# Stick-breaking attention: the earliest key block turned over and multiplied with V for 64 queries only

## The chip, the cores and the metric

The kernel runs on the 8 cores of one Trainium2 chip. The metric is the device time of the slowest core, in microseconds. Most executions agree within 0.3%. Some fall into a slower state, in which the cores of one die, or of both, are granted a lower clock; those executions are named slow, and only fast ones are compared with fast ones.

## The reference

One layer of a decoder: a SwiGLU half step, a short convolution beside stick-breaking attention, a second SwiGLU half step, an embedding gated per position, norms. Batch 4, sequence 8192, width 1024, 8 heads of 128. The part concerned is the attention:

```python
# A[t,s] = sigmoid(z_ts) * prod_{s<j<t} (1 - sigmoid(z_tj)), z = q.k / sqrt(dh), s < t
mask = k_pos[None, :] < q_pos[:, None]                      # strict causal
log_1m_beta = jnp.where(mask, jax.nn.log_sigmoid(-z), 0.0)
tail = lax.cumsum(log_1m_beta, axis=3, reverse=True) - log_1m_beta
a = jnp.where(mask, jnp.exp(jax.nn.log_sigmoid(z) + tail), 0.0)
out = jnp.einsum('bhqk,bhkd->bhqd', a, vf)
```

The weight of a key is what is left of a stick after all later keys have broken off their share. Each key leaves a factor 1 - sigmoid(z), so with the reference's random inputs nothing that fp32 can hold is left after some 200 keys. That is why the kernel need not look at all 8192 keys.

## The kernel before

A core computes half a sequence of one batch: 8 tiles of 512 positions. A slot is one head and one block of 128 queries; a core has 8 tiles x 8 heads x 4 blocks = 256 slots. Each slot looks at 320 keys: the 128 of its own block, the 128 before them, and 64 more. Slots are run as a pipeline of three stages between the matmuls of the large projections:

```python
WIN = 320
...
def attn1(self, s, q, kpieces, L, diag, init):
    ...                                  # scores: matmuls of q with L keys, into PSUM bank 4 or 5
    self.act(nbt.v(0, 0, L), z, AF.Sigmoid, scale=-QS)           # 1 - beta
    ...                                  # scan from the latest key to the earliest:
    #   rt = max(rt * (1 - beta), mask); mask row q is 1 where own-block key s >= q
    A = self.ats[s % 3]
    pad = -L % 128
    self.tt(A.v(0, pad, pad + L), Rt.v(0, 1, L + 1), Rt.v(0, 0, L), ALU.subtract)   # the weights
    return Rt.v(0, 0, 1)                 # what is left before the earliest key

def attn2(self, s, nb):                  # turn the weights over, 128 x 128 at a time
    T = self.PS[6]
    ...
    for b in range(nb):
        ins = self.nc.tensor.transpose(T[:, b * 128:(b + 1) * 128], A.v(0, b * 128, (b + 1) * 128).ap, self.ident.v(0).ap)
    ...
    self.act(self.att[s % 2].v(0, 0, nb * 128), View(T[:, 0:nb * 128], self.psres[6]), AF.Copy)

def attn3(self, s, vpieces, qb, start, stop, o):    # times V, summed over key blocks in PSUM
    ...
    for b, vv in enumerate(vpieces):
        ...
        ins = self.nc.tensor.matmul(O[:, qb * 128:(qb + 1) * 128], lhsT=vv.ap, rhs=at.v(0, b * 128, (b + 1) * 128).ap, ...)

def slot(self):
    ...
    end = b.attn1(s, X.q.v(h, qb * 128, (qb + 1) * 128), self.kpieces(X, h, qb), WIN, True, None)
    f = b.fend.v(0, self.base + s, self.base + s + 1)
    b.op(b.POOL, lambda: b.nc.gpsimd.tensor_copy(out=f.ap, in_=end.ap), [end], [f])
```

The 320 weights lie behind 64 columns of zeros, so that they fill three blocks of 128. The last two lines belong to a guard. For each slot GpSimd saves the column of what is left of the stick; before the end it is tested whether all of it is exactly zero. If one value is not, the whole layer is computed again with all keys:

```python
def flags():
    b.op(DVE, lambda: nc.vector.tensor_scalar(out=flg.v(0).ap, in0=b.fend.v(0).ap, scalar1=0.0, scalar2=None,
                                              op0=ALU.not_equal), [b.fend.v(0)], [flg.v(0)])
    ...                                  # maximum along the row, then a matmul with ones counts partitions
...
guard = nc.If(cond[0] >= 0) if force_general else nc.If(cond[0] > 0)
with guard:
    b.barrier()
    ...
    general(b, nc, S, A, B, x_d, p_d, out_d, h1_d, kT_d, v_d, uhalo, ring_off, at)
```

In this document the program up to the guard is the short path, and what the guard adds behind it, the computation with all keys, is the general path.

## Time and profile before

| | before |
|---|---|
| fast executions, with the first measurement | 3516.31, 3517.28, 3518.05 us |
| slow one, left out | 3659.46 us |
| TensorE busy | 97% of the span |
| attention: scores, transposes, V products | about 1% each of the chain that ended last |
| GpSimd busy | 6% |

The busy line, the chain, one slot on the timeline and the waits are shown in the prediction below. Two lines it does not show matter for the comparison. First the copy of the turned-over weights out of PSUM, from the page's groups (busy us, mean ns; then the idle time ahead and its releaser), then the guard's copies and test on core 3, from the list of the instructions on the guard's tile (duration in ns as smallest/median/largest, first and last start in us):

```profile
L281 ACT ACTIVATE sb_at_93<-ps 128x384 bf16<-128x384 bf16 x128 | 62.9, 491 | 158.5 <-PE ps L659 158.5
```

```profile
L741 POOL COPY sb_fend<-sb_rt_87 x128: 183/183/511, 384.4 to 3101.4; 128x1 f32<-128x1 f32 x128
...
L1189 DVE TENSOR_SCALAR sb_flg<-sb_fend x1: 286/286/286, 3117.7 to 3117.7; 128x256 bf16<-128x256 f32 x1
```

### The profile page before, as it was taken

Reading aid. Unit: us, or ns where it says so; the run is one execution under the profiler, and the core shown is the slowest. Engines: PE = TensorE matmul, PEld = TensorE weight load, DVE = VectorE, ACT = ScalarE, POOL = GpSimd, SP = SyncE. Lnnn points to the kernel's source line nnn. Section 1 sums busy time; section 2 is a strip of 40 time slices with the busy share of each in tenths; the row PEclk is TensorE's granted clock in tenths of the full one; section 3 lists DMA queues with packets and bytes.
Section 4 is the critical chain, followed back from the end, with each engine's and each line's share of the span. In section 5 each row is a group of like instructions: output and inputs, shape, how many; then the busy total and the mean of one; then the engine's idle time right before and its main releaser. Section 6 shows DMA issues by size and latency. Waiting matters only on the chain.

```text
span 3513.5 us, 50834 instructions; the slowest of 8 cores (3506.3 to 3513.5 us)
## 1 busy us (share of the span) xinstructions
PE 3401.3 (97%) x17714; PEld 1639.0 (47%) x17714; DVE 1564.1 (45%) x2461; ACT 1038.4 (30%) x2024; POOL 196.3 (6%) x479
## 2 busy tenths in 40 slices
PE   6999999999999999999999999999999999999995
PEld 3555545444444455444444444544444445544453
DVE  3224376522552367541544337652255236754234
ACT  3112424312331244321333142531233124432113
POOL 0000111100000000100000000010000000010000
PEclk9999999999999999999999999999999999999997
DMA  8565746786533321342223422152232332133231
GB/s 179 127 136 149 156 103 149 175 204 138 126 92 118 122 71 61 102 138 66 86 75 117 131 79 73 55 162 76 68 95 82 119 127 73 61 103 114 72 109 49
DMA packets 98817, 381.03 MB, mean 108 GB/s; under 512 B 11136, under 2 KB 16512, under 8 KB 93440
## 3 DMA queue, kind: packets, MB, share of 16 engines
q1 hardware_dynamic: 68304, 253.95, 21.8%
q0 software_dynamic: 30256, 123.75, 16.8%
q8 instruction: 150, 2.46, 0.3%
q14 instruction: 107, 0.88, 0.1%
HBM read 346.19 MB, written 93.85 MB: 125 GB/s over the span
## 4 chain that ended last, share of the span: by engine, by line
PE 93%; DVE 2%; ACT 2%; DMA 1%; issue 1%; DVEq 0%; SPq 0%; ACTq 0%; POOLq 0%
PE ps L253 85%; PE ps L271 5%; PE ps L673 1%; PE ps L659 1%; ACT L281 1%; PE ps L626 1%; DMA sb_xA<-x_in 0%; DMA sb_ring<-w_out 0%; DMA sb_ring<-w_in1g 0%; DMA sb_ring<-w_in1u 0%; DVE sb_t_80 L288 0%; DVE sb_hB L288 0%; DVE sb_rt_87 L646 0%; DVE sb_t_82 L288 0%; ACT sb_t_81 L281 0%
## 5 line engine op out<-in xcount | busy, mean ns | idle before, releaser
L253 PE MATMUL ps<-sb_uA,sb_ring 128*128 128x512 bf16 x4448 | 994.3, 380 | 18.0 <-DVE sb_phalo L285 8.4
L253 PE MATMUL ps<-sb_uB,sb_ring 128*128 128x512 bf16 x4448 | 990.3, 379 | 3.8 <-DVE sb_mB L285 2.8
L253 PEld LDWEIGHTS ps<-sb_uA,sb_ring 128*128 128x128 bf16 x4448 | 432.8, 98 | 525.3 <-issue 26.5
L253 PEld LDWEIGHTS ps<-sb_uB,sb_ring 128*128 128x128 bf16 x4448 | 433.6, 98 | 510.4 <-issue 7.1
L253 PE MATMUL ps<-sb_hidB,sb_ring 128*128 128x512 bf16 (+2 forms) x1584 | 312.8, 357 | 5.6 <-DVE sb_t_81 L288 5.6
L253 PE MATMUL ps<-sb_hidA,sb_ring 128*128 128x512 bf16 x1408 | 309.3, 379 | 0.5 <-DMA sb_ring<-w_out 0.5
L253 PEld LDWEIGHTS ps<-sb_hidB,sb_ring 128*128 128x128 bf16 x1584 | 149.3, 99 | 164.4 <-issue 6.4
L253 PEld LDWEIGHTS ps<-sb_hidA,sb_ring 128*128 128x128 bf16 x1408 | 137.7, 98 | 165.4 <-issue 1.0
L646 DVE TENSOR_TENSOR_SCAN sb_rt_87<-sb_nb_85,sb_mask 128x320 f32<-128x320 f32 x128 | 105.5, 824 | 210.9 <-ACT sb_nb_85 L281 186.4
L281 ACT ACTIVATE sb_t_81<-ps 128x512 f32<-128x512 f32 (+3 forms) x176 | 101.6, 578 | 271.2 <-PE ps L253 235.3
L281 ACT ACTIVATE sb_t_83<-ps 128x512 f32<-128x512 f32 (+3 forms) x175 | 101.3, 579 | 260.3 <-PE ps L253 244.8
L281 ACT ACTIVATE sb_t_80<-ps 128x512 f32<-128x512 f32 (+4 forms) x148 | 85.3, 576 | 257.9 <-PE ps L253 257.2
L281 ACT ACTIVATE sb_t_82<-ps 128x512 f32<-128x512 f32 (+3 forms) x147 | 84.4, 574 | 247.4 <-PE ps L253 247.4
L281 ACT ACTIVATE sb_sqA<-sb_hA 128x512 f32<-128x512 f32 x105 | 66.1, 629 | 289.3 <-DVE sb_accA L285 254.6
L281 ACT ACTIVATE sb_sqB<-sb_hB 128x512 f32<-128x512 f32 (+2 forms) x112 | 67.5, 602 | 273.7 <-DVE sb_accB L285 245.7
L646 DVE TENSOR_TENSOR_SCAN sb_rt_88<-sb_nb_86,sb_mask 128x320 f32<-128x320 f32 x128 | 105.3, 822 | 64.0 <-ACT sb_nb_86 L281 31.1
L253 PE MATMUL ps<-sb_mA,sb_ring 128*128 128x512 bf16 x512 | 116.4, 379 | 0.0
L281 ACT ACTIVATE sb_at_93<-ps 128x384 bf16<-128x384 bf16 x128 | 62.9, 491 | 158.5 <-PE ps L659 158.5
L281 ACT ACT_TABLE_LOAD x63 | 80.8, 1283 | 66.8 <-PE ps L253 43.8
L285 DVE TENSOR_TENSOR sb_hidB<-sb_t_80,ps 128x512 bf16<-128x512 f32 x47 | 32.3, 687 | 128.1 <-PE ps L253 110.6
L253 PE MATMUL ps<-sb_mB,sb_ring 128*128 128x512 bf16 x384 | 88.8, 379 | 0.0
L281 ACT ACTIVATE sb_at_92<-ps 128x384 bf16<-128x384 bf16 x128 | 62.5, 488 | 84.3 <-PE ps L659 83.1
(358 smaller groups left out, 3386.5 us busy)
## 6 DMA issues: line engine op xcount, KB each, us to landing
sb_ring<-wb_out SPq DMA_DIRECT2D x56, 704.0 KB, 4.3
sb_ring<-wb_in1g SPq DMA_DIRECT2D x33, 512.0 KB, 4.0
sb_ring<-wb_in1u SPq DMA_DIRECT2D x33, 512.0 KB, 4.0
sb_ring<-wb_in2g SPq DMA_DIRECT2D x33, 512.0 KB, 3.6
sb_ring<-wb_in2u SPq DMA_DIRECT2D x33, 512.0 KB, 4.4
sb_ring<-w_out POOLq DMA_DIRECT2D x16, 704.0 KB, 9.7
wb_out<-sb_ring SPq DMA_DIRECT2D x16, 704.0 KB, 6.4
h_s<-sb_hA POOLq DMA_DIRECT2D x8, 1024.0 KB, 5.9
```

Of the source, the lines that this page charges most:

```text
L253: ins = self.nc.tensor.matmul(ps.ap, lhsT=l.ap, rhs=r.ap, start=(t == 0), stop=(t == n - 1), skip_group_check=True)
L271: ins = self.nc.tensor.matmul(ps.ap, lhsT=l.ap, rhs=r.ap, start=(t == 0), stop=(t == n - 1), skip_group_check=True)
L281: self.op(self.ACT, lambda: self.nc.scalar.activation(out=out.ap, in_=in_.ap, func=func, scale=scale, **kw), [in_, *extra], [out])
L285: self.op(self.DVE, lambda: self.nc.vector.tensor_tensor(out=out.ap, in0=a.ap, in1=b.ap, op=alu), [a, b], [out])
L626: ins = self.nc.tensor.matmul(Z[:, c0:c0 + kv.ap.shape[-1]], lhsT=q.ap, rhs=kv.ap, start=(n == 0), stop=(n == len(kpieces) - 1), skip_grou ...
L646: self.op(self.DVE, lambda: self.nc.vector.tensor_tensor_scan(out=rv.ap, data0=nv.ap, data1=mv.ap, initial=iv, op0=ALU.mult, op1=ALU.max), ...
L659: ins = self.nc.tensor.transpose(T[:, b * 128:(b + 1) * 128], A.v(0, b * 128, (b + 1) * 128).ap, self.ident.v(0).ap)
L673: ins = self.nc.tensor.matmul(O[:, qb * 128:(qb + 1) * 128], lhsT=vv.ap, rhs=at.v(0, b * 128, (b + 1) * 128).ap, start=(start and b == 0), ...
```

## The change

Of the 64 earliest keys of a window, queries 64 to 127 of the block are to see nothing any more: they keep 256 keys and the first 64 queries keep 320. The block that holds the 64 earliest keys is then turned over for 64 queries, not 128, and multiplied with V for 64 columns. The transposes of the kernel before turn over whole blocks of 128 x 128; to turn over fewer queries, they become matmuls with the identity, of which 64 columns are used for that block. Scores, sigmoid, scan and subtraction stay at 320 keys.

The guard must follow: for queries 0 to 63 (partitions 0 to 63) what is left before column 0 has to be zero, for queries 64 to 127 what is left before column 64. So two columns are saved per slot, and each half of the partitions is tested on its own column.

```diff
+NQ = WIN - 256
-            if r == 6:
-                t = g.enter_context(nc.psum_tensor(f"ps{r}", [128, 1024], BF16))
   (bank 6 is fp32 like the others)
-        for b in range(nb):
-            ins = self.nc.tensor.transpose(T[:, b * 128:(b + 1) * 128], A.v(0, b * 128, (b + 1) * 128).ap, self.ident.v(0).ap)
+        for b, n in pieces:
+            ins = self.nc.tensor.matmul(T[:, c:c + n], lhsT=A.v(0, b * 128, (b + 1) * 128).ap,
+                                        rhs=self.ident.v(0, 0, n).ap, start=(c == 0), stop=True, skip_group_check=True)
+            c += n
 ...
-        self.act(self.att[s % 2].v(0, 0, nb * 128), View(T[:, 0:nb * 128], self.psres[6]), AF.Copy)
+        self.act(self.att[s % 2].v(0, 0, c), View(T[:, 0:c], self.psres[6]), AF.Copy)
 ...
-            ins = self.nc.tensor.matmul(O[:, qb * 128:(qb + 1) * 128], lhsT=vv.ap, rhs=at.v(0, b * 128, (b + 1) * 128).ap,
+            ins = self.nc.tensor.matmul(O[:, qb * 128:qb * 128 + n], lhsT=vv.ap, rhs=at.v(0, c, c + n).ap,
 ...
-        for blk in range(qb - 2, qb + 1):
+        for blk in (qb - 1, qb, qb - 2):
 ...
-            b.attn2(s - 2, 3)
+            b.attn2(s - 2, [(1, 128), (2, 128), (0, NQ)])
 ...
-            f = b.fend.v(0, self.base + s, self.base + s + 1)
-            b.op(b.POOL, lambda: b.nc.gpsimd.tensor_copy(out=f.ap, in_=end.ap), [end], [f])
+            for i, e in enumerate((end, b.rts[s % 2].v(0, NQ, NQ + 1))):
+                f = b.fend.v(i, self.base + s, self.base + s + 1)
+                b.op(b.POOL, lambda: b.nc.gpsimd.tensor_copy(out=f.ap, in_=e.ap), [e], [f])
 ...
-            b.op(DVE, lambda: nc.vector.tensor_scalar(out=flg.v(0).ap, in0=b.fend.v(0).ap, scalar1=0.0, scalar2=None,
-                                                      op0=ALU.not_equal), [b.fend.v(0)], [flg.v(0)])
+            for i, p in enumerate((slice(0, NQ), slice(NQ, 128))):
+                b.op(DVE, lambda: nc.vector.tensor_scalar(out=flg.v(0).ap[p], in0=b.fend.v(i).ap[p], scalar1=0.0,
+                                                          scalar2=None, op0=ALU.not_equal), [b.fend.v(i)], [flg.v(0)])
```

More of the change, by code (lines that the diff above doesn't have):

```diff
@@ L135, in __init__ @@
         for r in range(8):
-            if r == 6:
-                t = g.enter_context(nc.psum_tensor(f"ps{r}", [128, 1024], BF16))
-            else:
-                t = g.enter_context(nc.psum_tensor(f"ps{r}", [128, 512], F32))
-            self.PS.append(t)
+            self.PS.append(g.enter_context(nc.psum_tensor(f"ps{r}", [128, 512], F32)))
             self.psres.append([self.newres()])
@@ L651, in attn1, with attn2 @@
         return Rt.v(0, 0, 1)
-    def attn2(self, s, nb):
+    def attn2(self, s, pieces):
         T = self.PS[6]
@@ L657, in attn2 @@
         self.waits(PE, [A.v(0).res], [self.psres[6]])
-        for b in range(nb):
-            ins = self.nc.tensor.transpose(T[:, b * 128:(b + 1) * 128], A.v(0, b * 128, (b + 1) * 128).ap, self.ident.v(0).ap)
+        c = 0
+        for b, n in pieces:
+            ins = self.nc.tensor.matmul(T[:, c:c + n], lhsT=A.v(0, b * 128, (b + 1) * 128).ap,
+                                        rhs=self.ident.v(0, 0, n).ap, start=(c == 0), stop=True, skip_group_check=True)
+            c += n
         ins.then_inc(PE.sem, 1)
@@ L670, in attn3 @@
         self.waits(PE, [at.v(0).res], [self.psres[7]])
-        for b, vv in enumerate(vpieces):
+        c = 0
+        for b, (vv, n) in enumerate(vpieces):
             self.waits(PE, [vv.res], [])
-            ins = self.nc.tensor.matmul(O[:, qb * 128:(qb + 1) * 128], lhsT=vv.ap, rhs=at.v(0, b * 128, (b + 1) * 128).ap,
+            ins = self.nc.tensor.matmul(O[:, qb * 128:qb * 128 + n], lhsT=vv.ap, rhs=at.v(0, c, c + n).ap,
                                         start=(start and b == 0), stop=(stop and b == len(vpieces) - 1),
@@ L676, in attn3 @@
             self.record(PE.sem, PE.cnt + 1, [vv.res], [])
+            c += n
         ins.then_inc(PE.sem, 1)
@@ L723, in vpieces @@
                 t, r = self.A.v, 4 + blk
-            out.append(t.v(r, h * 128, (h + 1) * 128))
+            out.append((t.v(r, h * 128, (h + 1) * 128), NQ if blk == qb - 2 else 128))
         return out
@@ L1025, in build @@
         b.phalo = at("phalo", KC, 16, F32)
-        b.fend = at("fend", 1, NTILE * 32, F32)
+        b.fend = at("fend", 2, NTILE * 32, F32)
         flg = at("flg", 1, NTILE * 32, BF16)
@@ L1318, in full_attention @@
                                [(kall.v(0, lo * 128, hi * 128), 0)], nb * 128, first, init)
-                b.attn2(s, nb)
-                b.attn3(s, [vall.v(r) for r in range(lo, hi)], qb, qb == 0 and first, qb == 3 and lo == 0, X.q.v(h))
+                b.attn2(s, [(r, 128) for r in range(nb)])
+                b.attn3(s, [(vall.v(r), 128) for r in range(lo, hi)], qb, qb == 0 and first, qb == 3 and lo == 0, X.q.v(h))
                 first = False
```

## The prediction

> **What bounds the kernel now.** I read the whole-span busy table first, then the chain that ended last, then the rows of the attention instructions, then one stretch of the timeline inside attention.
>
> ```profile
> PE 3401.3 (97%) x17714; PEld 1639.0 (47%) x17714; DVE 1564.1 (45%) x2461; ACT 1038.4 (30%) x2024; POOL 196.3 (6%) x479
> PE 93%; DVE 2%; ACT 2%; DMA 1%; issue 1%; DVEq 0%; SPq 0%; ACTq 0%; POOLq 0%
> PE ps L253 85%; PE ps L271 5%; PE ps L673 1%; PE ps L659 1%; ACT L281 1%; PE ps L626 1%; DMA sb_xA<-x_in 0%; DMA sb_ring<-w_out 0%; DMA sb_ring<-w_in1g 0%; DMA sb_ring<-w_in1u 0%; DVE sb_t_80 L288 0%; DVE sb_hB L288 0%; DVE sb_rt_87 L646 0%
> ```
>
> The first line (busy microseconds, share of the span, instructions) says that the tensor engine is busy 97% of the time and no other engine half of it. A busy share alone would not prove a bound, so the next two lines matter more: the chain that ended last runs through the tensor engine for 93% of the span, 85% of it in the one helper of the large projections (L253). The attention's own three lines, the scores (L626), the transposes (L659) and the product with V (L673), carry about 1% each. That caps the whole subject: the change touches L659 and L673 alone, so even deleting both could not give more than 2 or 3%.
>
> How large the two are, I take from the timeline of the tensor engine in one attention step (a "slot"; columns: start us, us, engine, line, operation, tiles, shape, count):
>
> ```profile
> start us, us, engine line op out<-in xcount [idle before <-releaser]
> 409.03 0.33 PE L673 MATMUL ps<-sb_at_92,sb_vA 128*128 128x128 bf16 x3
> 409.20 0.33 PE L659 MATMUL ps<-sb_ident,sb_a_91 128*128 128x128 bf16 x3
> 409.37 0.19 PE L626 MATMUL ps<-sb_ck,sb_qA 128*128 128x64 bf16 x1
> 409.39 0.27 PE L626 MATMUL ps<-sb_kA,sb_qA 128*128 128x256 bf16 x1
> 409.50 1.89 PE L253 MATMUL ps<-sb_uB,sb_ring 128*128 128x512 bf16 x8
> ```
>
> The durations overlap, because matmuls are pipelined: a 128-column one is recorded as 219 ns long, yet three of them (409.03 to 409.20) hold the engine for 0.17 us. What counts is start to start. From the start times of all matmuls of this core (core 3) I take the medians: 56 ns after a 128-column L659 or L673, 82 ns after 192 columns, 110 after 256, 136 after 320, 216 after 512, and 28 ns after a 64-column one. The last is the important figure, since the change makes 64-column matmuls; it comes from the 64 score matmuls of that width (409.37 to 409.39 is one of them), each with a weight load of its own before it and another before its successor. L659 has 768 starts that sum to 43.0 us, L673 768 that sum to 44.5 us, so both together hold the engine 87.5 us, 2.5% of the span.
>
> Is the engine free to go faster there? The waits of the tensor engine put only these on the two lines:
>
> ```profile
> PE ps L673 <- ACT sb_at_93 L281: 3.6, 6, 0.6
> PE ps L673 <- ACT sb_at_92 L281: 3.3, 5, 0.9
> PE ps L659 <- DVE sb_a_90 L285: 1.3, 1, 1.3
> ```
>
> These are us in total, times, and the longest: 12 waits in 256 slots. They are in the drains at the end of each pass over two tiles, where slots run without projection work between them. In all other slots the engine never waits, so a shorter matmul moves everything after it forward.
>
> **What the Trainium skill says.** "TensorE: Matmul & The Clock Gate", section "Wait — 56ns, not 53.3ns?", gives start to start of a warm array as N / 2.4 GHz + about 2.5 ns, never below about 25 ns. That is 55.8 ns for 128 columns and 29.2 for 64; the trace has 56 and 28, so it agrees. The section "Part 4: PE-mode transpose" of the same page puts a 128x128 transpose at 275 to 390 ns and says that it does not count as activity for the clock. The trace does not agree on the cost: the transposes follow each other every 56 ns and are recorded at 219 ns, exactly like the V matmuls beside them. So replacing the transpose mode by an ordinary matmul with the identity should neither cost nor gain. "PSUM — Partial Sum Buffer", section "Specifications (TRN2)", says that matmuls write fp32 and transposes the input's type; this is why the change makes that bank fp32, and no run here has shown it yet. "ScalarE: Activation LUTs", section "What ACT_TABLE_LOAD costs", gives 0.833 ns per column for an activation beside a fixed part. The trace agrees: the copy of 128x384 has a median of 491 ns and the sigmoid of 128x320 one of 437, which is 54 ns for 64 columns.
>
> **The change part by part.** A core has 8 tiles x 8 heads x 4 query blocks = 256 slots.
>
> 1. Transposes: three of 128 columns become matmuls with the identity of 128, 128 and 64 columns. The stationary operand is still the block of attention weights and the loads of it stay at three. Saved per slot: 56 - 28 = 28 ns. On the path.
> 2. V products: three of 128 columns become 128, 128 and 64, with the earliest block last so that the accumulation begins with a full-width write. Again 28 ns per slot, on the path.
> 3. Sum on the path: 256 x 2 x 28 ns = 14.3 us. With the measured means (56.0 and 28.3 ns) it is 14.2 us.
> 4. ScalarE copies 320 fp32 columns instead of 384 bf16 ones: an estimate from the row above is 437 ns for 491, so 256 x 54 ns = 13.8 us less. ScalarE is busy 30% and this lies beside other work. Only in the drains does the copy stand on the path: 4 passes x about 3 slots x 54 ns = 0.6 us gained. The 56 ns that those slots save on the tensor engine is lost in the same waits, 12 x 56 ns = 0.7 us. I put the two against each other: zero.
> 5. GpSimd copies two columns of the remaining product for each slot, not one: 256 x 183 ns (median of the copy before) = 46.8 us more, POOL from 6% to about 7%. Its copies follow the scan and hold a buffer that the scan of two slots later overwrites; slots start 2.2 us apart (scans at 408.41 and 410.61), so a release 0.18 us later meets a deadline some 3 us off. Nothing on the path. GpSimd also starts the weight transfers of the first pass, which may leave 0.2 us later; the ring is filled several slabs ahead, so I count nothing.
> 6. The final flag test is two vector instructions instead of one: one more of about 286 ns, once, while projections run. Nothing.
> 7. Order: compared instruction by instruction, the five queues keep their order; only shapes change, and POOL gets its second copy. No slot moves, since slots are placed by counted projection matmuls, not by time.
>
> Scores (L626), sigmoid, scan and subtraction stay at 320 keys. 3517.3 - 14.2 = 3503.1 us; I say 3503.
>
> **A question of correctness that would also be one of time.** Queries 64 to 127 now drop the earliest block, which is right only if their remaining product is zero before it; otherwise the flag sends the kernel into its general path, which recomputes everything at a multiple of the time. The shortest run of keys is 192 in both kernels (query 0 with five half blocks, query 64 with four). I computed the log of the remaining product on the host in double precision for all queries: the largest is -128.1 both before and after, and fp32's smallest number is at -103.3. The general path is not taken.
>
> **The rivals.**
>
> *Weight loads become the bound.* A load is recorded as 98 ns, longer than a 28 ns matmul, so two 64-column matmuls might be paced by loads: the gain would be 0 and the time 3517. Against it: those 64 score matmuls start their successor, which has a load of its own, 28 ns later; and the 2-column matmuls of the convolution halo, each with its own load, follow every 25 ns. For it: only that in the new order the 64-column matmul ends a group and its successor's load waits on another engine's semaphore. In the trace, the successors of L673 start after 56 ns at the median too, so such semaphores have long come. I give this 7%.
>
> *The ordinary matmul is dearer or cheaper than the transpose.* If fp32 results took longer to write, 512 full-width ones at a few ns would take back 1 or 2 us: 3505. The V matmuls write fp32 at 56 ns, so I doubt it. 5%.
>
> *The gain turns into a wait.* Slots are 56 ns shorter, and vector engine and ScalarE must keep up. In the first attention stretch (380 to 470 us) DVE is busy 54 of 90 us and ACT 38 of 90, so 2.5% less room does not make either the bound. It could lengthen a few existing waits, for the vector engine's convolution work (8.4 us on L253 for sb_phalo): up to 3 us back, 3506. 15%.
>
> *The gain is twice as large.* It would need the other full-width matmuls to shrink too; nothing does that.
>
> **Range and chances.** The undisturbed runs of before lie at 3516.3, 3517.3 and 3518.2 us, so noise is about 1 us, while waits that differ by chance between builds may be some 5 us. Half the gain gives 3510, and the gain plus a few lucky waits 3497: range 3497 to 3511. The gain is 0.4%, far within 2%. Faster by over 2% (70 us) is impossible by the cap on the two lines; slower by over 2% would need the general path or only disturbed executions.
>
> **What would show it.** In the changed kernel: start to start of 28 ns after the 256 new L659-type and 256 new L673-type matmuls of 64 columns, and both lines' sums near 36 and 37 us; still 56 ns after the identity matmuls of 128 columns; the copy of 128x320 at about 437 ns; 512 copies on POOL; tensor engine waits on the two lines still about 12. I am wrong if the 64-column ones hold the engine much over 30 ns, if the waits grow by several us, or if the general path runs.

## More of the kernel before

The mask, whose row q belongs to query q, does not come from code on the chip: it is part of an input array of constants, one row to a partition.

The guard is cheap: 256 copies, 183 ns at the median and about 510 at most, on an engine that is 6% busy, and one test of 286 ns, 400 us before the end.

## The result, and the profile after

| | before | after |
|---|---|---|
| executions of the first measurement | 3516.31, 3517.28, 3518.05 us (3659.46 slow) | 29025.96, 29264.2, 28897.38, 29255.81 us |
| ratio of fast runs | | 8.28 [8.20, 8.35] |

A ratio here is the mean time of one kernel's fast runs over that of the other's of the same rounds, so not quite the ratio of the medians.

The kernel took eight times as long. The page of the profile says where at once. First the span, the busy line, the tenths of the tensor engine and of its clock in 40 slices, then the chain by engine, then a costly group each of the vector engine, the tensor engine and ScalarE:

```profile
span 29024.3 us, 223779 instructions; the slowest of 8 cores (28887.5 to 29024.3 us)
...
PE 13593.6 (47%) x67434; PEld 6148.9 (21%) x67434; DVE 9937.8 (34%) x17471; ACT 6278.3 (22%) x12417; POOL 328.1 (1%) x807
...
PE   9999988523622622262236222622244222532225
...
PEclk8999988655755755575557555755566555755556
...
PE 46%; DVE 25%; ACT 15%; issue 9%; DMA 3%; DVEq 1%; ACTq 1%; POOLq 0%; SPq 0%; POOL 0%
...
L643 DVE TENSOR_TENSOR_SCAN sb_rt_88<-sb_nb_86,sb_rt_87,sb_mask 128x384 f32<-128x384 f32 (+1 forms) x2000 | 2002.8, 1001 | 5725.4 <-ACT sb_nb_86 L278 5725.4
...
L658 PE MATMUL ps<-sb_ident,sb_a_89 128*128 128x128 bf16 x4404 | 692.7, 291 | 3704.1 <-DVE sb_rt_88 L641 1788.7
...
L278 ACT ACTIVATE sb_at_93<-ps 128x384 bf16<-128x384 f32 (+3 forms) x2240 | 1077.2, 481 | 5556.7 <-PE ps L658 5556.7
```

The tensor engine has 67434 matmuls, where before had 17714: other work ran. Its tenths are at 9 in the first five slices, an eighth of the span, and mostly at 2 to 6 after that. The scans of 384 columns whose inputs include the preceding scan's buffer (`sb_rt_88<-...sb_rt_87`) exist only in the general path, where one group of keys continues the previous one. The windows of core 0 split the two (window; its length; busy us and instructions of PE, PEld, DVE, ACT, POOL; granted clock; DMA share; GB/s):

```profile
0.00:3545.00 3545.00, 3395.56 (x17483) 1635.16 (x17823) 1577.41 (x2483) 1037.08 (x2043) 283.33 (x735) 0.99 0.38 110
3545.00:28896.00 25351.00, 10027.48 (x49203) 4480.15 (x49612) 8352.67 (x14988) 5239.84 (x10375) 44.62 (x72) 0.59 0.12 40
```

The short path ran to its end, nearly as fast as it should, and then 25.35 ms of general path followed, in which scan, ScalarE and tensor engine wait for each other. All 8 cores have spans from 28887 to 29024 us, so all of them took it. The guard's test is on the timeline of core 5 (start us, us, engine, line, operation, tiles):

```profile
3251.15 0.60 DVE L1195 TENSOR_SCALAR sb_flg<-sb_fend 64x256 bf16<-64x256 f32 x2
3251.86 0.42 DVE L1197 TENSOR_REDUCE sb_flm<-sb_flg 128x1 f32<-128x256 bf16 x1
```

Nothing is odd in it: two half tests, 0.60 us together, then the maximum. A trace shows when the test ran, not what it found. What it found is the whole question.

The part that the change was meant for can be read in the same trace, in the 3.5 ms of short path: start to start after the 256 64-column identity matmuls the median is 28 ns, after the 64-column V products 28 ns, after the 128-column ones 56 ns. So before any experiment it was known that the time was saved and that the guard had fired. That first measurement carries no comparison of the output.

### The profile page after: what moved, and what is told of

It is laid out like the page before. It is cut to its first block, busy times and chain, and to the rows that moved or that the text cites. A ratio compares the mean times of both kernels' runs of the same rounds, so it can differ in the third digit from the quotient of the medians.

```text
span 29024.3 us, 223779 instructions; the slowest of 8 cores (28887.5 to 29024.3 us)
## 1 busy us (share of the span) xinstructions
PE 13593.6 (47%) x67434; PEld 6148.9 (21%) x67434; DVE 9937.8 (34%) x17471; ACT 6278.3 (22%) x12417; POOL 328.1 (1%) x807
## 4 chain that ended last, share of the span: by engine, by line
PE 46%; DVE 25%; ACT 15%; issue 9%; DMA 3%; DVEq 1%; ACTq 1%; POOLq 0%; SPq 0%; POOL 0%
PE ps L250 27%; DVE sb_rt_88 L643 7%; DVE sb_rt_87 L643 7%; PE ps L658 7%; PE ps L675 7%; PE ps L623 5%; ACT sb_at_93 L278 4%; ACT sb_nb_86 L278 4%; ACT sb_nb_85 L278 4%; ACT sb_at_92 L278 4%; DVE sb_a_91 L282 3%; DVE sb_a_90 L282 3%; DVE sb_a_89 L282 3%; DMA sb_vall<-v_s 2%; DVEq L190 1%
## 5 line engine op out<-in xcount | busy, mean ns | idle before, releaser
L250 PE MATMUL ps<-sb_uA,sb_ring 128*128 128x512 bf16 x17504 | 4039.2, 391 | 97.0 <-DVE sb_uA L285 71.3
L643 DVE TENSOR_TENSOR_SCAN sb_rt_88<-sb_nb_86,sb_rt_87,sb_mask 128x384 f32<-128x384 f32 (+1 forms) x2000 | 2002.8, 1001 | 5725.4 <-ACT sb_nb_86 L278 5725.4
L643 DVE TENSOR_TENSOR_SCAN sb_rt_87<-sb_nb_85,sb_rt_88,sb_mask 128x384 f32<-128x384 f32 (+1 forms) x1968 | 1969.7, 1001 | 5600.9 <-ACT sb_nb_85 L278 5600.9
L658 PE MATMUL ps<-sb_ident,sb_a_89 128*128 128x128 bf16 x4404 | 692.7, 291 | 3704.1 <-DVE sb_rt_88 L641 1788.7
L658 PE MATMUL ps<-sb_ident,sb_a_90 128*128 128x128 bf16 x4389 | 690.7, 291 | 3686.9 <-DVE sb_rt_88 L641 1765.5
L658 PE MATMUL ps<-sb_ident,sb_a_91 128*128 128x128 bf16 x4391 | 690.4, 291 | 3686.8 <-DVE sb_rt_88 L641 1757.5
L623 PE MATMUL ps<-sb_kall,sb_qA 128*128 128x384 bf16 (+2 forms) x4224 | 2183.3, 517 | 351.5 <-DMA sb_kall<-kT_s 351.5
L278 ACT ACTIVATE sb_at_93<-ps 128x384 bf16<-128x384 f32 (+3 forms) x2240 | 1077.2, 481 | 5556.7 <-PE ps L658 5556.7
L278 ACT ACTIVATE sb_at_92<-ps 128x384 bf16<-128x384 f32 (+2 forms) x2240 | 1076.9, 481 | 5479.0 <-PE ps L658 5477.8
L250 PEld LDWEIGHTS ps<-sb_uA,sb_ring 128*128 128x128 bf16 x17504 | 1742.1, 100 | 2308.2 <-issue 535.4
L675 PE MATMUL ps<-sb_at_92,sb_vall 128*128 128x128 bf16 x6208 | 993.4, 295 | 1588.9 <-ACT sb_at_92 L278 1506.4
L675 PE MATMUL ps<-sb_at_93,sb_vall 128*128 128x128 bf16 x6208 | 993.1, 295 | 1577.7 <-ACT sb_at_93 L278 1517.8
L278 ACT ACTIVATE sb_nb_85<-ps 128x384 f32<-128x384 f32 (+2 forms) x2240 | 1077.4, 481 | 2428.2 <-PE ps L623 2428.0
L278 ACT ACTIVATE sb_nb_86<-ps 128x384 f32<-128x384 f32 (+3 forms) x2240 | 1076.6, 481 | 2423.4 <-PE ps L623 2423.3
L658 PEld LDWEIGHTS ps<-sb_ident,sb_a_89 128*128 128x128 bf16 x4404 | 349.4, 117 | 4329.4 <-issue 4329.4
L658 PEld LDWEIGHTS ps<-sb_ident,sb_a_91 128*128 128x128 bf16 x4391 | 348.7, 117 | 4311.3 <-issue 4311.3
L658 PEld LDWEIGHTS ps<-sb_ident,sb_a_90 128*128 128x128 bf16 x4389 | 348.2, 117 | 4311.7 <-issue 4311.7
```

Source lines behind the costliest of these rows:

```text
L250: ins = self.nc.tensor.matmul(ps.ap, lhsT=l.ap, rhs=r.ap, start=(t == 0), stop=(t == n - 1), skip_group_check=True)
L278: self.op(self.ACT, lambda: self.nc.scalar.activation(out=out.ap, in_=in_.ap, func=func, scale=scale, **kw), [in_, *extra], [out])
L623: ins = self.nc.tensor.matmul(Z[:, c0:c0 + kv.ap.shape[-1]], lhsT=q.ap, rhs=kv.ap, start=(n == 0), stop=(n == len(kpieces) - 1), skip_grou ...
L643: self.op(self.DVE, lambda: self.nc.vector.tensor_tensor_scan(out=rv.ap, data0=nv.ap, data1=mv.ap, initial=iv, op0=ALU.mult, op1=ALU.max), ...
L658: ins = self.nc.tensor.matmul(T[:, c:c + n], lhsT=A.v(0, b * 128, (b + 1) * 128).ap, rhs=self.ident.v(0, 0, n).ap, start=(c == 0), stop=Tr ...
L675: ins = self.nc.tensor.matmul(O[:, qb * 128:qb * 128 + n], lhsT=vv.ap, rhs=at.v(0, c, c + n).ap, start=(start and b == 0), stop=(stop and ...
```

## The experiments

Eighteen kernels ran on chips 2, 6, 10 and 11. All gave correct outputs. Each was run beside the kernel before on its own chip. The unaltered changed kernel was run again only as the 17th, and it took the short path. The sixteen runs ahead of it altered the guard and were first read as if the alteration had mattered.

### The arithmetic, with the old guard

*e1_col0*: both columns are still saved, but only column 0 is tested, on all 128 partitions, with the one instruction of the kernel before. As a guard it is too weak for queries 64 to 127; the outputs are correct with these inputs.

```diff
-            for i, p in enumerate((slice(0, NQ), slice(NQ, 128))):
-                b.op(DVE, ... out=flg.v(0).ap[p], in0=b.fend.v(i).ap[p] ...)
+            b.op(DVE, ... out=flg.v(0).ap, in0=b.fend.v(0).ap ...)
```

> The changed kernel with only its final test put back as it was: column 0 of the remaining product, all 128 queries, one instruction. The second copy is still made but not tested. Theory (the test on the second saved column is what fires, the arithmetic is as predicted): the short path is taken and the time is 3503 us, between 3497 and 3511. Rival (the new matmuls or copies corrupt something that the flag sees, or the fp32 bank slows the attention): the general path again, 29000 us, or the short path at 3517 us or more.

Measured in 5 rounds: fast runs 3504.79, 3504.49, 3502.17, 3506.82, 3503.8 us, mean 3504.4 (two slow ones, 3579.13 and 4177.81, left out); before in the same rounds 3518.89, 3519.25, 3516.56, 3516.82, 3517.91, mean 3517.9 (six slow ones left out). That is 13.5 us less, ratio 0.9961 [0.9946, 0.9977]. The gain that was predicted is there, short path throughout.

### Is it the test of one half?

*e2_masked128* has the condition of the change by instructions on all 128 partitions, each multiplied by a column of zeros and ones, then the maximum of the two:

```diff
+            for i, (o, m) in enumerate(((flg, pm0), (flg1, pm1))):
+                b.op(DVE, ... out=o.v(0).ap, in0=b.fend.v(i).ap, scalar1=0.0, scalar2=m.ap, op0=ALU.not_equal, op1=ALU.mult ...)
+            b.tt(flg.v(0), flg.v(0), flg1.v(0), ALU.max)
```

> The changed kernel with the same condition (column 0 for queries 0-63, column 64 for queries 64-127) but tested by instructions over all 128 partitions, each multiplied by a 0/1 column, and a maximum of the two. Theory A (the saved column holds a nonzero value for some query from 64 on): general path, about 29000 us. Theory B (the instruction that starts at partition 64 doesn't test what it should): short path, about 3503 us.

3505.06 us (and one slow, 3788.13): short path.

*e3_low_only* fills the upper half of the flags with zeros and makes the lower half's test alone:

```diff
-            for i, p in enumerate((slice(0, NQ), slice(NQ, 128))):
+            b.op(DVE, lambda: nc.vector.memset(flg.t[64:128, 0, :], 0.0), [], [flg.v(0)])
+            for i, p in enumerate((slice(0, NQ),)):
```

> The changed kernel with the test of queries 64-127 replaced by zeros (memset), the half-partition test of queries 0-63 kept. Theories A and B (what fires is the upper half) both: short path, about 3503 us. Rival (half-partition tests fire wherever they start, or column 0 is disturbed): general path, about 29000 us.

3503.88 us (and one slow, 3879.42): short path.

*e4_threshold* keeps both half tests but asks for more than 1e-30 in place of not zero:

```diff
-   scalar1=0.0, ... op0=ALU.not_equal
+   scalar1=1e-30, ... op0=ALU.is_gt
```

> The changed kernel, its two half-partition tests asking for more than 1e-30 in place of unequal to zero. If what fires is a tiny remainder (smaller than fp32's normal numbers or near them): short path, about 3503 us. If it is a value of another origin (garbage, a value of an unfinished scan, not a number): general path, about 29000 us.

3506.14 us (and one slow, 4054.53): short path.

*f1_high_only* is the mirror image of e3: lower flags zero, upper half's test on column 64 alone.

```diff
+            b.op(DVE, lambda: nc.vector.memset(flg.t[0:64, 0, :], 0.0), [], [flg.v(0)])
+            b.op(DVE, ... out=flg.v(0).ap[64:128], in0=b.fend.v(1).ap[64:128], scalar1=0.0, op0=ALU.not_equal ...)
```

> The half-partition test of queries 64-127 alone (column 64, partitions 64-127); the lower half of the flags is a memset of zeros. If this instruction by itself looks at the wrong place: general path, about 29000 us. If it only goes wrong behind the test of the lower half, which is the instruction just ahead of it in the changed kernel: short path, about 3503 us.

3527.28 us, where before took 3541.15 on the same chip; in each, two cores of one die had a granted clock of 0.982. Short path. The upper half's test alone found nothing.

*f2_low_rows_zeroed* keeps the tests but first writes zeros over the partitions 0 to 63 of the second saved column, which no test should read:

```diff
+            b.op(DVE, lambda: nc.vector.memset(b.fend.t[0:64, 1, :], 0.0), [], [b.fend.v(1)])
```

> Both half-partition tests as in the changed kernel, but partitions 0-63 of the second saved column (values that no right test looks at) are set to zero first. If the test of partitions 64-127 in truth reads partitions 0-63: short path, about 3503 us. If it reads something else, or writes its result wrongly: general path, about 29000 us.

3525.5 us: short path.

*f3_high_tests_col0* keeps two half tests, both on column 0:

```diff
-   in0=b.fend.v(i).ap[p]
+   in0=b.fend.v(0).ap[p]
```

> Two half-partition tests, both of the first saved column, which is zero in all 128 partitions (the run with the test of column 0 took the short path). If the upper test reads other partitions of the same column: short path, about 3503 us. If it leaves garbage in the upper half of the flags, or reads neighbouring memory: general path, about 29000 us.

3530.05 us: short path.

*f4_unmasked* is a control that gives a flag on purpose: column 64 tested on all 128 partitions, also those of queries 0 to 63, which have only 128 to 191 keys behind them there.

```diff
+            b.op(DVE, ... out=flg.v(0).ap[0:128], in0=b.fend.v(1).ap[0:128], scalar1=0.0, op0=ALU.not_equal ...)
```

> A control: one test of the second saved column in all 128 partitions. It is nonzero in some of partitions 0-63 (queries with 128 to 191 keys behind column 64; the host's arithmetic in fp32 has about 1100 of 16384 on one core, the largest 1.4e-37), so the general path, about 29000 us, under every theory in which wrongly read lower partitions are the cause. If it takes the short path, the lower partitions hold zeros on the chip and cannot be what fired.

29133.76 us, and one slow at 29627.44: general path. The page's first line has the same shape as in the first measurement:

```profile
span 29132.0 us, 223777 instructions; the slowest of 8 cores (29001.6 to 29132.0 us)
```

The instruction count is two short of that of the first measurement. So partitions 0 to 63 of the second column do hold values that are not zero on the chip, and one test that reads them costs all this time. That made a test reading the wrong half look likely.

### Is it the pair of half tests?

*g1_swapped* makes the upper half's test first:

```diff
+            for i, p in (((1, slice(NQ, 128)), (0, slice(0, NQ)))):
```

> The changed kernel with the two half-partition tests in the other order: queries 64-127 first, then 0-63. If the second of the two instructions picks up what belongs to the first's partitions, it is now the lower test that goes to partitions 64-127 of column 0, which are zero: short path, about 3503 us. If the first is disturbed by the second's addresses, it is the upper test that sees column 0, zero again: short path as well. If merely having both is wrong, whatever the order: general path, about 29000 us.

3503.31 us: short path.

*g2_wait_between* lets the vector engine wait for the first test to finish before the second:

```diff
+            b.wait(DVE, DVE.sem, DVE.cnt)
```

> The changed kernel with one wait added: the test of queries 64-127 starts only when the test of queries 0-63 has signalled its end. If the two instructions disturb each other by overlapping: short path, about 3503 us. If the second is wrong even after the first has ended: general path, about 29000 us.

3505.65 us: short path.

*g3_low_unused* writes the lower test into a tile that nobody reads and zeros the lower flags:

```diff
+            b.op(DVE, lambda: nc.vector.memset(flg.t[0:64, 0, :], 0.0), [], [flg.v(0)])
+            b.op(DVE, ... out=flg1.v(0).ap[0:64], in0=b.fend.v(0).ap[0:64] ...)
+            b.op(DVE, ... out=flg.v(0).ap[64:128], in0=b.fend.v(1).ap[64:128] ...)
```

> Both tests back to back as in the changed kernel, but the first (queries 0-63) writes its result to a tile that nothing reads; the lower half of the flags is a memset of zeros ahead of both. If the second instruction is the one that goes wrong: general path, about 29000 us. If the first is disturbed by the second that follows it: short path, about 3503 us.

3508.78 us: short path.

*g4_first_half_zeroed* is f2 for the first 128 of the 256 slots only:

```diff
+            b.op(DVE, lambda: nc.vector.memset(b.fend.t[0:64, 1, 0:128], 0.0), [], [b.fend.v(1)])
```

> As the run with the lower partitions of the second saved column set to zero, but only its first 128 of 256 columns. If only the beginning of the instruction reads the wrong partitions: short path, about 3503 us. If all of it does, or its end, or if it is the first test's end that reads the second column: general path, about 29000 us.

3502.51 us: short path. Half of the slots still had values of the kind that f4 shows not to be all zero, and nothing was flagged.

*h1_memset_ahead* leaves the change alone and only adds an unused vector instruction ahead of the tests:

```diff
+            b.op(DVE, lambda: nc.vector.memset(flg1.t[0:64, 0, :], 0.0), [], [flg1.v(0)])
```

> Control: the changed kernel with a memset of an unused tile on partitions 0-63 ahead of its two tests, nothing else. If a memset ahead does not matter: general path, about 29000 us, and the three earlier runs with a memset ahead mean what they seemed to mean. If it takes the short path (3503 us): those three say nothing about where the wrong value comes from.

3528.24 us: short path.

*h2_clear_low*, *h3_clear_high* and *h4_clear_low_head* make both tests as in the change and then clear a part of the flags: the lower half, the upper half, or the lower half of the first 64 slots.

```diff
+            b.wait(DVE, DVE.sem, DVE.cnt)
+            b.op(DVE, lambda: nc.vector.memset(flg.t[0:64, 0, 0:256], 0.0), [], [flg.v(0)])      # h2
+            b.op(DVE, lambda: nc.vector.memset(flg.t[64:128, 0, 0:256], 0.0), [], [flg.v(0)])    # h3
+            b.op(DVE, lambda: nc.vector.memset(flg.t[0:64, 0, 0:64], 0.0), [], [flg.v(0)])       # h4
```

> The changed kernel, but when both tests have ended, the flags of partitions 0-63 are set to zero before they are reduced. If the first test (queries 0-63) is the one with the wrong result: short path, about 3503 us. If the wrong flags lie in partitions 64-127: general path, about 29000 us.

> The same with the flags of partitions 64-127 set to zero. If the second test (queries 64-127) is wrong: short path, about 3503 us. If the first is wrong: general path, about 29000 us. One of this and the run before should take the short path, unless both halves are wrong.

> The same with the flags of partitions 0-63 set to zero in their first 64 columns alone. If the wrong flags are the lower half's and come from where the two instructions meet, at the head of the flags: short path, about 3503 us; if at their tail or all over, or in the upper half: general path, about 29000 us.

h2: 3503.43 us (and one slow, 3628.88). h3: 3526.3 us (and one slow, 3711.56). h4: only slow executions, 3655.17, 3888.88 and 4187.43 us, which is still far from 29000: short path in all three runs. The one execution of before, 3602.55 us, was slow too, so these times are not compared with it. h2 and h3 between them clear every flag once, so wherever a false flag had stood, one of them should have gone the long way. Neither did. With that, the theory that a pair of half-partition tests is misread fell: no alteration had kept the flag, which suggested that none had removed it.

### The unaltered kernel again

*i1_again* is the changed kernel to the byte, 3 rounds.

> The changed kernel itself, to the byte. If the pair of half-partition tests is wrong whenever it stands as it does: general path in every execution, about 29000 us. If what sent the four executions of the first measurement into the general path depends on the chip or on what its memory held before: short path in some or all executions, at 3503 us, ratio 0.996 to the kernel before.

Short path 6 times of 6: fast 3503.48, 3509.47 and 3532.22 us, slow 3851.15, 4088.45 and 4157.72 (one or both dies at a granted clock of 0.82 to 0.92 in those). Before in the same rounds: 3515.56, 3517.26, 3537.99, 3548.47 fast, 3672.03 and 4154.1 slow. Ratio 0.9975 [0.9865, 1.0084], wide because in one fast run of the changed kernel and two of before a pair of cores had a granted clock near 0.98; by itself it does not show the gain, which rests on e1. The page of its fastest execution:

```profile
span 3499.2 us, 50756 instructions; the slowest of 8 cores (3490.0 to 3499.2 us)
...
PE 3369.1 (96%) x17378; PEld 1624.8 (46%) x17714; DVE 1563.3 (45%) x2462; ACT 1025.0 (29%) x2024; POOL 283.3 (8%) x735
...
PE 92%; DVE 3%; ACT 2%; issue 2%; DMA 1%; DVEq 0%; ACTq 0%; SPq 0%; POOLq 0%
```

The tests on the timeline of core 3 have the durations and spacing of those of the first measurement, to the hundredth of a microsecond:

```profile
3100.97 0.60 DVE L1195 TENSOR_SCALAR sb_flg<-sb_fend 64x256 bf16<-64x256 f32 x2
3101.68 0.42 DVE L1197 TENSOR_REDUCE sb_flm<-sb_flg 128x1 f32<-128x256 bf16 x1
```

The test of core 5 above started 150 us later; core 5 had a granted clock of 0.95 in the first 3499 us of that execution. On core 0, at 0.99, it started at 3102.3 us there and at 3103.5 here. On cores 3 and 5 the tensor engine, vector engine, ScalarE and GpSimd also carry out the same instructions in the same order in both executions, with the same lines, tiles and shapes, to the end of the short path (17714 matmuls). So the program, the order of the test and its timing are the same in an execution that went the long way and in one that did not. What differed, as far as these traces show, must lie in the tested values.

*j1_poison* asks whether that could be old contents of memory: all five tiles of the test are filled with ones at the start.

```diff
+        for t in (b.fend, flg, flm, flb, fli):
+            b.op(DVE, lambda t=t: nc.vector.memset(t.t[:, :, :], 1), [], [t.ks(0, t.K)])
```

> The changed kernel with its saved columns, flags, maximum, count and the count's integer form all set to 1 at the start; nothing else is altered. If old contents of these tiles reach the decision (a flag not written, or read too early): general path, about 29000 us, in all executions. If every value is written in time: short path, 3503 us, ratio 0.996 of the fast runs to the kernel before, and the cause of the first measurement's general path is not in old contents of these tiles.

Short path 6 of 6 on a fourth chip: fast 3506.57, 3531.5, 3531.37, 3531.23, 3532.1 us (in the last four, cores at a granted clock of 0.982), slow 3762.35; before 3515.53, 3516.53 and 3542.03 to 3548.69 when fast. Ratio 0.9968 [0.9913, 1.0023]. In these six executions everything that the guard reads was therefore written in time; what the tiles had held before made no difference.

## Why the prediction was right or wrong

**Right: the gain of the two shorter matmuls.** On core 3 the sum of start to start for the turning over went from 43.0 to 36.0 us (28.8 for 512 matmuls of 128 columns, 7.3 for 256 of 64), where I said near 36; for the V products from 44.5 to 37.5 us (28.6 and 9.0), where I said near 37. The median is 28 ns after a 64-column matmul and 56 after a 128-column one. One slot on the timeline of the tensor engine of core 3 in i1_again, to be set against that of the prediction:

```profile
409.93 0.22 PE L675 MATMUL ps<-sb_at,sb_cv 128*128 128x128 bf16 x1
409.98 0.22 PE L675 MATMUL ps<-sb_at,sb_vA 128*128 128x128 bf16 x1
410.04 0.19 PE L675 MATMUL ps<-sb_at,sb_cv 128*128 128x64 bf16 x1
410.07 0.31 PE L658 MATMUL ps<-sb_ident,sb_a 128*128 128x128 bf16 x3
410.21 0.30 PE L623 MATMUL ps<-sb_kA,sb_qA 128*128 128x320 bf16 x1
```

The three V products start at 409.93 and the next line at 410.07: 0.14 us, where it was 0.17. The three matmuls of L658 take 0.14 to the scores, 0.17 before (the row names only the form of the first). The measured gain with the short path is 13.5 us (e1_col0), the prediction's sum was 14.2. The two rivals on the tensor engine are out: weight loads do not pace the 64-column matmuls, and an identity matmul into fp32 takes the 56 ns of the transpose.

**Right: the waits stay.** The attention's two lines in the tensor engine's waits (us, times, longest) have 11 and 1 waits, 12 as before; the third is the convolution wait that the prediction feared would grow:

```profile
PE ps L675 <- ACT sb_at L278: 6.3, 11, 0.9
PE ps L658 <- DVE sb_a L282: 1.4, 1, 1.4
...
PE ps L250 <- DVE sb_phalo L282: 8.6, 6, 2.0
```

The first sum was 3.6 + 3.3 = 6.9 us in before and is 6.3; the third was 8.4 and is 8.6. All waits in the list of core 3 sum to 87.3 us, 89.8 before, so the rival that the gain turns into a wait is out as well. The 64-column V products sum to 9.0 us, 35 ns in the mean beside a median of 28, almost wholly because of the single wait on the second line: it falls behind the last V product, which is now the 64-column one (1569 ns to the next start at 521 us). Before, it fell behind a 128-column one (1508 ns).

**Right: ScalarE.** The copy has 320 columns and takes the 437 ns that were estimated:

```profile
L278 ACT ACTIVATE sb_at<-ps 128x320 bf16<-128x320 f32 x256 | 111.6, 436 | 238.9 <-PE ps L658 237.7
```

**Mis-sized, without effect: GpSimd.** I took 183 ns for each second copy and said 7% busy. It is 8%:

```profile
L746 POOL COPY sb_fend<-sb_rt 128x1 f32<-128x1 f32 x512 | 155.9, 336 | 788.8 <-DVE sb_rt L643 787.9
```

The mean is 336 ns because the first of the two takes 183 ns at the median and the second 459. The timeline shows the neighbour:

```profile
410.57 0.58 POOL L746 COPY sb_fend<-sb_rt 128x1 f32<-128x1 f32 x2 [1.92 <-DVE sb_rt L643]
410.61 0.49 DVE L282 TENSOR_TENSOR sb_a<-sb_rt 128x320 bf16<-128x320 f32 x1 [0.17 <-PE ps L623]
```

The second copy runs while the vector engine subtracts two columns of the same buffer. "GPSIMD Engine Reference", section "1. Specifications", says that GpSimd shares its SBUF interfaces with VectorE and contends with vector instructions that have two SBUF inputs. The subtraction is one, and the trace of core 3 agrees: all 182 second copies that overlapped a subtraction by more than 50 ns finished 40 to 46 ns after it, while the 37 that ran beside a vector instruction with one operand in PSUM took 178 to 181 ns. The 183 ns that I took from before was a median there too, over copies of up to 513 ns. The scan that overwrites the buffer still came at least 764 ns after the second copy (1512 before), so nothing was on the path, as the prediction said.

**Wrong: the step "The general path is not taken."** The prediction put it on the sentence that the shortest run of keys is 192 in both kernels, and on the largest log of -128.1 that followed from it. The figure itself is right: a recalculation gives -128.1 for both kernels, with the mask in its place. For the reference's inputs the step held in every execution of the experiments: the changed kernel itself and its poisoned form took the short path 12 times of 12, on two chips. In the four executions of the first measurement it did not hold, on any core, and that alone is the factor of 8.28: 25.35 ms of general path behind 3.5 ms of short path. Why it did not hold stays open; what follows says what the runs exclude and what is left.

What the runs show for the inputs and chips that they had is that none of these gives a flag: half-partition tests as such (e3, f1, f3), their order and spacing (g1, g2, h1), their results being misread (h2, h3), an upper half with values that are not zero (f1, with column 64 and not zero as the test), and old contents of the test's tiles (j1). Since i1 took the short path too, none of them can tell what flagged the first measurement; they only show that no such fault is a steady one. The instructions up to the branch and the timing around the test are the same in both kinds of execution.

What fits all of it was computed on the host only and **is not shown on the chip**. The sentence about 192 keys in both kernels is true only if the mask's rows lie on the partitions of their queries. In the kernel before, a partition with mask row j has 192 + j keys behind column 0, whatever j is, so never fewer than 192. In the changed kernel a partition of the upper half has 128 + j keys behind column 64; that is 192 or more only if j is 64 or more. The old guard's margin did not depend on which row of the mask a partition got, the new one's does. In an fp32 calculation of the attention with every input array rotated by half of its first axis (the mask's rows displaced by 64), the changed kernel's test finds values on 22 partitions on the even cores and 25 on the odd ones, so on all 8, and the kernel before's on none. With the constants alone displaced by 64 rows, core 1 again has 25; the recalculation gives the same numbers, and 24 to 27 on each of the 8 cores for the constants alone, with none for the kernel before. With the arrays displaced by one row, or the constants by 8 or 32, so that partition p gets row p - 8 or p - 32, the changed kernel's test finds none on core 1. In the other direction, in which the last partitions get the first rows, the recalculation finds 1, 8 and 21 partitions there for 1, 8 and 32 rows. If the first measurement ran with arrays that were not the reference's in such a way, its outcome follows: 8 cores flagged in every execution, with the kernel before untroubled beside it. One run agrees with the picture, though it does not prove it: f4 shows that runs of 128 to 191 keys leave values that are not zero on the chip, as the calculation has it, which on core 1 finds such values in 1106 of the 16384 entries of partitions 0 to 63 of the second column, none above 1.4e-37. Other values behind a mask in its place are a poorer candidate, though also untested: the shortest run of keys is then 192 in both tests, so what is left behind 192 keys would be expected to send the kernel before the long way too. Other causes in the chip or the run of the first measurement cannot be excluded, and the run that would decide, the changed kernel with displaced constants, was not made.

**The range and the chances.** 3497 to 3511 us holds the undisturbed short path: e1's fast runs lie between 3502 and 3507, and the two of i1 with every core at a granted clock of 0.988 or more at 3503 and 3509. The prediction named the general path as what would make the kernel slower, and as a sign of being wrong, but gave it no chance of its own beside the 7, 5 and 15% of its rivals. That was too little for a step whose failure costs a factor of eight and that had been checked with one set of inputs in double precision, without asking on what else the new guard's margin rests.

**A version that beats both.** On the short path the changed kernel is that version, by the 0.4% that e1 shows with the old test; with its own test i1 gives 0.9975 [0.9865, 1.0084], which agrees but does not show it. Keeping its two tests while making the mask on the chip from the partition number would free the guard of the input array; this was not built.

## What to carry to other kernels

A guard that can send a kernel into a slow path is part of its time: before narrowing it, work out for each row what margin it keeps and which inputs and layouts that margin rests on, since a margin that was uniform can become one that hangs on a table's order. When a measured disaster has to be explained, run the unaltered kernel again first; fifteen alterations were read here as cures for something that was no longer there. In this kernel a matmul with its own weight load held the engine 56 ns with 128 columns and 28 ns with 64, so columns that nobody needs were worth cutting, even though a transpose had to become an identity matmul.

## What the Trainium skill lacked or had wrong

- "TensorE: Matmul & The Clock Gate", section "Part 4: PE-mode transpose", gives 275 to 390 ns as the duration of a 128x128 transpose and no start to start. Here a transpose between other matmuls was recorded at 219 ns and held the engine 56 ns start to start, and the identity matmul in its place the same 219 and 56 ns.
- The same page, section "Back-to-back issue gap", says of streams of weight load and matmul that N=128 takes about 81 ns each and N=512 about 131. The runs show 56 and 216 ns, with a weight load for each, as the formula gives that the section calls one for isolated matmuls, and 28 ns for 64 columns.
- No page has the point that a branch to a slow path, taken or not by the values computed, has to be counted in a prediction, here 25.35 ms behind 3.5 ms.
